# Nine portions of the attention issued beside the second query slab, and weights of feature-major slabs ordered seven pieces ahead

## The chip, the core and the metric

The kernel runs on one core of one Trainium2 chip. The metric is the device time of one execution in microseconds. A core has five engines with queues of their own: TensorE (PE in the profile; its weight loads are PEld), VectorE (DVE), ScalarE (ACT), GpSimd (POOL) and SyncE (SP), which here issues all transfers. They synchronise through semaphores, and each works through its own instructions in the order in which the program put them.

## The reference, cut to what matters

Two layers of a decoder trunk over 512 tokens of width 1024. Each layer normalises its input, multiplies it by one wide matrix, feeds two groups of heads from the columns of the product, and projects their joined outputs back:

```python
h = rms_norm(x, g_pre)
proj = jnp.einsum('bsd,de->bse', h, w_in)
q_h, f_h, i_h, z_h, q_a, k_a, v_a, z_a = jnp.split(proj, SPLIT_POINTS, axis=-1)
o_h = hgrn2(q_h, f_h, i_h, lb)                       # gated linear recurrence, 8 heads of 128
o_h = rms_norm(o_h, g_head).reshape(B, S, HG_WIDTH) * silu(z_h)
q_a = rotary(q_a ...); k_a = rotary(k_a ...)
o_a = sliding_window_attention(q_a, k_a, v_a, sinks) * silu(z_a)
y = jnp.einsum('bse,ed->bsd', jnp.concatenate([o_h, o_a], axis=-1), w_out)
return x + rms_norm(y, g_post)
```

The attention has 16 query heads of width 64, in groups of eight that share one of two key and value heads. A query sees the last 128 keys, itself included, and a learned sink per head joins the softmax. It is computed in blocks of 128 queries against the 256 keys of their own block and the one before.

## The kernel before, in words

**Arithmetic.** All is float32. A weight or activation that enters a projection is split into a rounded high part and the rest, `hi` and `lo`, and `mm3` (lines 174 to 177) multiplies three combinations, so that one step of a projection is three matmuls of 128x128 by 128x512.

**Weights.** They come in pieces of 128x512 (256 KB). `w_load` (147) issues a piece's transfer on SP into one of three `raw` buffers; `w_conv` (156) casts it on ScalarE into `whi` (169) and subtracts on VectorE into `wlo` (170; for the first query slab and the keys and values every second subtraction is on GpSimd). There are nine buffers of each. A slab is eight pieces.

**Slabs and their order.** `ORDER` lists them: keys and values (`kv`), two query slabs (QA, QA+1), two slabs of inputs (IV, IV+1), then FQ slabs (forget gates and queries of two HGRN2 heads each) between gates (ZA, ZH) and pieces of the output projection. A slab is a row of `Unit`s. In a feature-major slab (the queries, FQ and ZA) the weights are the stationary operand, and each of the four units uses two pieces for its eight steps, so that buffers come free one after the other. In a token-major slab (IV, ZH, kv) all pieces serve each of the four units, and they come free only in the last one.

**Steps.** `step` (211) issues one `mm3` of the unit whose turn it is. When the one active unit is half done, a second one is started beside it and they take turns; three PSUM buffers (`pj`) hold their results. After each step `w_conv` is told how far to have ordered casts: to the beginning of the next slab, plus one piece per four steps done (in slabs of 32 steps), plus `LEAD`, 4. A unit's end calls its evacuation.

**Attention.** The evacuation of a query slab (`qa_stream`, 371) multiplies by cosines and sines on VectorE (378 to 385), combines on GpSimd (388, 389), splits into high and low (391, 392), stores both to a `stack` in DRAM and loads them back restacked into `qs[g]` (394, 397), for one of four groups `g` of four heads per two units. The tiles of `qs` have two buffers. `att_stream` (489) runs over 16 pairs of group and block of queries, and issues, with a `yield` after each portion: the scores of block i (`att_scores`: eight matmuls, masking and maxima on VectorE, exponentials on ScalarE, the product with the reciprocal sums on GpSimd), the transposes of block i−2 (`att_transpose`, with a selection by mask on GpSimd), and the values of block i−4 (`att_value`). That makes 48 portions.

**Interleaving.** `merge` (45) takes streams with a total each and always goes on with the one that has the smallest share of its total behind it. In `run` (769) steps are issued until all four groups of queries exist, two more steps follow, and then the attention, with a total of 50, is merged with the steps that remain through the first FQ slab. The HGRN2 heads follow in the same way, two by two.

**Who sets the order.** The order in which the Python code issues instructions is a priority. A scheduler at compile time gives each engine its sequence by simulating the engines, so that an instruction whose operands or buffers are not ready there can be overtaken by a later one. Matmuls that are wrapped in `pin` (all of the attention and of HGRN2) keep their issued order among one another on TensorE; those of `mm3` are not pinned.

Of the kernel before, what the change touches and what calls it, by code (L numbers as in the profile page):

```python
# [20 lines left out]
NT = SEQ // 128  # L21
KT = D_MODEL // 128
# [5 lines left out]
FLOOR = 1e-20  # L28
NSLAB = 12
QA, IV, FQ, ZA, ZH = 0, 2, 4, 8, 10  # L30

W_BUFS = 9
RAW_BUFS = 3
# [2 lines left out]
DEFER = 18  # L36
PJ, SC = 3, 3
LEAD = 4
POOL_SLABS = (QA,)
FB = 8  # L40
QB = 4
# [3 lines left out]
def merge(*streams):  # L45
    live = [[g, 0.0, float(total)] for g, total in streams]
    while live:
        s = min(live, key=lambda e: e[1] / e[2])
        try:
            s[1] += next(s[0]) or 1.0  # L50
        except StopIteration:
            live.remove(s)


def chain(*gens):
    for g in gens:
        yield from g


def drain(g):  # L60
    for _ in g:
        pass
# [3 lines left out]
def hybrid_kernel(ctx: ExitStack, tc: tile.TileContext, x, wkv, win, wout, g_pre, g_post, lbp, ghead, sinks,  # L66
# [15 lines left out]
    def pj():  # L82
        return ps.tile([P, 512], F32, tag="pj", name="pj", bufs=PJ)
# [51 lines left out]
    for key, (first, n) in slab_first.items():  # L135
        if key[0] == "kv" or key[2] in POOL_SLABS:
            on_pool.update(range(first, first + n))
    kv_pieces = {slab_first["kv", l][0] + j: l for l in range(DEPTH) for j in range(KT // 2)}
    kv_room = {0}
    ahead = {("kv", l): sum(slab_first["out", l - 1, "h1"]) for l in range(1, DEPTH)}  # L140
    for l in range(DEPTH - 1):
        ahead["out", l, "h1"] = sum(slab_first["out", l, "h1"]) - KT - LEAD
    raws = {}
# [3 lines left out]
    def w_load(n):  # L147
        while state["raw"] < min(n, len(pieces)):
            i = state["raw"]
            src = pieces[i]  # L150
            t = wp.tile([P, 512], F32, tag="raw", name="raw", bufs=RAW_BUFS)
            nc.sync.dma_start(t.rearrange("p (a c) -> p a c", a=2) if len(src.shape) == 3 else t, src)
            raws[i] = t
            state["raw"] += 1

    def w_conv(n):
        w_load(n)
        while state["conv"] < min(n, len(pieces)):
            i = state["conv"]
            if i in kv_pieces and kv_pieces[i] not in kv_room:  # L160
                return
            w_load(i + RAW_BUFS)
            v = raws.pop(i)
            if i in kv_pieces:
                hi, lo = (big.tile([P, 512], F32R, tag="v", name="wkv", bufs=8) for _ in range(2))
            else:
                hi = wp.tile([P, 512], F32R, tag="whi", name="whi")
                lo = wp.tile([P, 512], F32R, tag="wlo", name="wlo")
            nc.scalar.copy(hi, v)  # L169
            (nc.gpsimd if i in on_pool and i % 2 else nc.vector).tensor_tensor(lo, v, hi.bitcast(F32), op=ALU.subtract)  # L170
            conv[i] = (hi, lo)
            state["conv"] += 1

    def mm3(o, sta, mov, start, stop):
        nc.tensor.matmul(o, lhsT=sta[1], rhs=mov[0], start=start, stop=False)  # L175
        nc.tensor.matmul(o, lhsT=sta[0], rhs=mov[1], start=False, stop=False)  # L176
        nc.tensor.matmul(o, lhsT=sta[0], rhs=mov[0], start=False, stop=stop)  # L177
# [8 lines left out]
    def run_first():  # L186
        _, key, fn = waiting.pop(0)
        fn()
        emitted.add(key)

    def ensure(key):
        while key not in emitted:
            run_first()
# [8 lines left out]
    units, active, turn, slab_steps, slab_done = deque(), [], [0], {}, {}  # L202
# [8 lines left out]
    def step():  # L211
        if not active or (len(active) == 1 and units and 2 * (len(active[0].ks) - active[0].i) <= len(active[0].ks)):
            u = units.popleft()
            first, n = slab_first[u.key]
            w_conv(first + n)
            u.w = [conv[first + j] for j in range(n)]
            for key in u.needs:
                ensure(key)
            u.o = pj()[:, 0:u.ncol]
            active.append(u)  # L220
        u = active[turn[0] % len(active)]
        turn[0] += 1
        k = u.ks[u.i]
        mm3(u.o, u.sta(k, u.w), u.mov(k, u.w), u.i == 0, u.i == len(u.ks) - 1)
        u.i += 1
        for e in waiting:
            e[0] -= 1
        while waiting and waiting[0][0] <= 0:
            run_first()
        slab_done[u.key] += 1  # L230
        first, n = slab_first[u.key]
        w_conv(ahead.get(u.key, first + n) + slab_done[u.key] * KT // slab_steps[u.key] + LEAD)
        if u.i == len(u.ks):
            active.remove(u)
            u.evac(u.o)

    def remaining(key):
        return sum(len(u.ks) - u.i for u in list(active) + list(units) if slab_first[u.key][0] <= slab_first[key][0])

    def through(key):  # L240
        while slab_done[key] < slab_steps[key]:
            step()
            yield 1.0

    def until(cond):
        while not cond():
            step()
# [76 lines left out]
    def layer(l, last):  # L324
# [44 lines left out]
        qs = {}  # L369
# [82 lines left out]
        def att_transpose(g, n, pt, odd):  # L452
            T = sc()
            for h in range(4):
                pin(nc.tensor.transpose(T[:, h * P:(h + 1) * P], pt[:, h * P:(h + 1) * P], ident))  # L455
            tt_ = tmp("a", F32R, 2)
            split_psum(tt_[:, 0], tt_[:, 1], T)
            if n == 0:
                return [(n, tt_[:, 0]), (n, tt_[:, 1])]
            terms = []  # L460
            for which in range(2):
                if which == 0:
                    d = big.tile([P, 2, 512], F32R, tag="oy", name="pcur", bufs=6) if odd else tmp("b", F32R, 2)
                else:
                    d = big.tile([P, 2, 512], F32R, tag="q", name="pprev", bufs=QB)
                sg = -1 if which == 0 else 1
                nc.gpsimd.affine_select(out=d.rearrange("p a (h t) -> p (a h) t", h=4),
                                        in_=tt_.bitcast(F32).rearrange("p a (h t) -> p (a h) t", h=4),
                                        pattern=[[0, 8], [-sg, P]], compare_op=ALU.is_ge, fill=0.0,
                                        base=-which, channel_multiplier=sg)  # L470
                terms += [(n - which, d[:, 0]), (n - which, d[:, 1])]
            return terms
# [16 lines left out]
        def att_stream(steps):  # L489
            pts, terms = {}, {}  # L490
            n = len(steps)
            for tt in range(NT):
                ensure(("k", l, tt))
            for i in range(n + VLAG):
                if i < n:
                    until(lambda: steps[i][0] in qs)
                    pts[i] = att_scores(*steps[i])
                    yield 1.0
                if 2 <= i <= n + 1:
                    terms[i - 2] = att_transpose(*steps[i - 2], pts.pop(i - 2), i % 2)  # L500
                    yield 1.0
                if i >= VLAG:
                    att_value(*steps[i - VLAG], terms.pop(i - VLAG))
                    yield 1.0
# [264 lines left out]
        def run():  # L769
            hg = lambda a: (hgrn(a), HG_N)  # L770
            rest = lambda key: (through(key), remaining(key))
            until(lambda: 3 in qs)
            for _ in range(2):
                step()
            merge((att_stream([(g, n) for g in range(4) for n in range(NT)]), 50), rest(("in", l, FQ)))
            merge(hg(0), rest(("in", l, FQ + 1)))
            merge(hg(2), rest(("in", l, FQ + 2)))
            merge(hg(4), rest(("out", l, "a1")))
            merge(hg(6), rest(("out", l, "h0")))
            kv_room.add(l + 1)  # L780
            drain(through(("out", l, "h1")))
# [129 lines left out]
```

## Time and profile before

| | |
|---|---|
| median of three runs | 956.77 us (952.09 to 960.68) |
| the profiled execution | 954.91 us, its span 953.2 us |
| TensorE busy | 918.9 us, 96% |
| VectorE busy | 681.9 us, 72% |
| ScalarE busy | 475.2 us, 50% |
| GpSimd busy | 267.3 us, 28% |
| mean granted TensorE clock | 0.989 |
| HBM read, written | 87.52 MB, 12.58 MB |

The span is the stretch from the first to the last instruction of the program in one profiled execution. Busy times are unions of instructions' durations. In the rows of the profile, L169 is line 169 of the kernel; a group's row ends with the idle time of its engine just before its instructions and with what ended it; in a row of the order of time the same stands in brackets. A row of the windows gives, for a stretch of the span, the busy time and the number of instructions of each engine, then the granted clock of TensorE as a share of full speed, the share of the DMA engines and GB/s. SPq is the queue of transfers on SyncE.

### The profile page before, as it was taken

The page shows a single profiled execution, that of the slowest core. Times are in us where ns is not written, and L with a number is a line of the kernel's source. Part 1 is how long each engine was busy: PE and PEld are TensorE (multiplying, and loading weights), DVE is VectorE, ACT ScalarE, POOL GpSimd, SP SyncE. Part 2 cuts the span into 40 slices and gives each one's busy share as a digit, 9 for nine tenths or more (in the row PEclk, how much of TensorE's full clock was granted, in tenths as well). Part 3 has the DMA queues.
Part 4 walks back from the last instruction along what each step waited for, and adds up shares of the span by engine and source line. Part 5 has one row for each costly group of instructions (what it writes and reads, how often), then busy time and mean ns, then how long its engine had stood idle before and what let it go on. Part 6 is the DMA issues. An engine that isn't in the chain of part 4 may idle for free.

```text
span 953.2 us, 19110 instructions
## 1 busy us (share of the span) xinstructions
PE 918.9 (96%) x7228; PEld 754.8 (79%) x7228; DVE 681.9 (72%) x1382; ACT 475.2 (50%) x1135; POOL 267.3 (28%) x282
## 2 busy tenths in 40 slices
PE   7999998999999999999969989989999999999996
PEld 5887887778878788788868878877788887887885
DVE  5866878796766685865795678778867578749546
ACT  5524766836464462434553257677363645414242
POOL 2232454422231221311331235434322213113102
PEclk8999999999999999999999999999999999999999
DMA  6456622232222332323443665122222233413313
GB/s 219 145 177 175 186 72 79 66 90 68 78 79 81 87 112 89 112 69 118 132 158 123 178 180 150 54 70 67 90 67 69 88 89 84 129 55 103 89 46 132
DMA packets 56716, 101.34 MB, mean 106 GB/s; under 512 B 6448, under 2 KB 8880, under 8 KB 56624
## 3 DMA queue, kind: packets, MB, share of 16 engines
q1 hardware_dynamic: 56624, 100.12, 35.5%
q8 instruction: 57, 0.93, 0.4%
q14 instruction: 35, 0.29, 0.1%
HBM read 87.52 MB, written 12.58 MB: 105 GB/s over the span
## 4 chain that ended last, share of the span: by engine, by line
PE 77%; DVE 9%; ACT 6%; issue 4%; POOL 2%; DMA 1%; SPq 0%; DVEq 0%; POOLq 0%; ACTq 0%
PE pj L175 22%; PE pj L177 21%; PE pj L176 21%; DVE wlo L170 3%; ACT s L442 2%; PE sc L583 2%; PE sc L428 2%; PE ac L652 1%; PE ac L481 1%; PE ac L640 1%; ACT whi L169 1%; PE ac L655 1%; DVE xn L306 1%; PE sc L455 1%; PE sc L700 1%
## 5 line engine op out<-in xcount | busy, mean ns | idle before, releaser
L169 ACT CAST whi<-raw 128x512 fp32r<-128x512 f32 x256 | 158.2, 620 | 193.5 <-PE pj L177 154.3
L170 DVE TENSOR_TENSOR wlo<-raw,whi 128x512 fp32r<-128x512 f32 x248 | 185.4, 753 | 63.0 <-ACT whi L169 61.0
L175 PE MATMUL pj<-hhi,wlo 128*128 128x512 f32 x512 | 206.4, 403 | 0.0
L177 PE MATMUL pj<-hhi,whi 128*128 128x512 f32 x512 | 200.8, 392 | 0.0
L176 PE MATMUL pj<-hlo,whi 128*128 128x512 f32 x512 | 200.2, 391 | 0.0
L177 PEld LDWEIGHTS pj<-hhi,whi 128*128 128x128 f32 x512 | 96.6, 189 | 21.0
L175 PEld LDWEIGHTS pj<-hhi,wlo 128*128 128x128 f32 x512 | 96.6, 189 | 18.7
L176 PEld LDWEIGHTS pj<-hlo,whi 128*128 128x128 f32 x512 | 96.8, 189 | 18.2
L175 PE MATMUL pj<-whi,hlo 128*128 128x512 f32 x256 | 103.2, 405 | 3.6 <-ACT whi L169 3.6
L175 PE MATMUL pj<-whi,ops 128*128 128x512 f32 x256 | 103.8, 406 | 0.0
L176 PE MATMUL pj<-wlo,hhi 128*128 128x512 f32 x256 | 100.4, 392 | 0.0
L177 PE MATMUL pj<-whi,ops 128*128 128x512 f32 x256 | 100.1, 391 | 0.0
L177 PE MATMUL pj<-whi,hhi 128*128 128x512 f32 x256 | 100.1, 391 | 0.0
L176 PE MATMUL pj<-wlo,ops 128*128 128x512 f32 x256 | 99.7, 390 | 0.0
L601 POOL TENSOR_TENSOR k<-k,tot 128x256 f32<-128x256 f32 x80 | 65.0, 832 | 109.9 <-PE sc L583 64.0
L175 PEld LDWEIGHTS pj<-whi,hlo 128*128 128x128 f32 x256 | 48.2, 188 | 12.6 <-ACT whi L169 4.5
L449 POOL TENSOR_TENSOR s<-s,sums 128x512 f32<-128x512 f32 x32 | 34.9, 1091 | 81.9 <-DVE sums L447 34.3
L177 PEld LDWEIGHTS pj<-whi,ops 128*128 128x128 f32 x256 | 48.0, 188 | 10.7
L600 DVE TENSOR_TENSOR q<-q,tot 128x256 f32<-128x256 f32 x80 | 46.9, 614 | 13.1 <-PE sc L583 8.6
L177 PEld LDWEIGHTS pj<-whi,hhi 128*128 128x128 f32 x256 | 48.1, 188 | 10.1
L175 PEld LDWEIGHTS pj<-whi,ops 128*128 128x128 f32 x256 | 48.1, 188 | 9.3
L176 PEld LDWEIGHTS pj<-wlo,ops 128*128 128x128 f32 x256 | 48.2, 188 | 9.0
(172 smaller groups left out, 1587.0 us busy)
## 6 DMA issues: line engine op xcount, KB each, us to landing
raw<-in_win_dram SPq DMA_DIRECT2D x192, 256.0 KB, 2.7
raw<-in_wout_dram SPq DMA_DIRECT2D x64, 256.0 KB, 2.7
stack<-rot SPq DMA_DIRECT2D x16, 512.0 KB, 3.9
qs<-stack SPq DMA_DIRECT2D x32, 256.0 KB, 4.4
a<-in_x_dram SPq DMA_DIRECT2D x12, 256.0 KB, 3.1
raw<-in_wkv_dram SPq DMA_DIRECT2D x8, 256.0 KB, 4.0
x_mid<-a SPq DMA_DIRECT2D x8, 256.0 KB, 2.1
a<-x_mid SPq DMA_DIRECT2D x8, 256.0 KB, 3.2
```

The source lines that it names most:

```text
L169: nc.scalar.copy(hi, v)
L170: (nc.gpsimd if i in on_pool and i % 2 else nc.vector).tensor_tensor(lo, v, hi.bitcast(F32), op=ALU.subtract)
L175: nc.tensor.matmul(o, lhsT=sta[1], rhs=mov[0], start=start, stop=False)
L176: nc.tensor.matmul(o, lhsT=sta[0], rhs=mov[1], start=False, stop=False)
L177: nc.tensor.matmul(o, lhsT=sta[0], rhs=mov[0], start=False, stop=stop)
L306: nc.vector.scalar_tensor_tensor(xn, xt[c], r, g[c], op0=ALU.mult, op1=ALU.mult)
L428: pin(nc.tensor.matmul(S[:, h * 256:(h + 1) * 256], lhsT=q[:, 2 * hp_ + h, t_], rhs=kst[v][p][:, (n - 1) * P:(n + 1) * P], start=(h == 0 a ...
L442: nc.scalar.activation(pt[:, h * P:(h + 1) * P], cur[h], AF.Exp, bias=negm[:, h:h + 1], scale=SCALE, accum_out=sums[:, h:h + 1])
L449: nc.gpsimd.tensor_tensor(pv, pv, sums.unsqueeze(2).broadcast_to([P, 4, P]), op=ALU.mult)
L583: pin(nc.tensor.matmul(L[32 * b:32 * b + 32, c:c + 16], lhsT=k[:, o_:o_ + 32], rhs=qv[:, blk:blk + qu, 1, :], start=True, stop=True, tile_ ...
L600: nc.vector.tensor_tensor(qv[:, :, 1, :], qv[:, :, 1, :], tv[:, :, 0].unsqueeze(2).broadcast_to([P, nb, hh]), op=ALU.mult)
L601: nc.gpsimd.tensor_tensor(kv_[:, :, 0, :], kv_[:, :, 0, :], tv[:, :, 1].unsqueeze(2).broadcast_to([P, nb, hh]), op=ALU.mult)
```

## The change

Attention starts when the first query slab has delivered its two groups (`1 in qs`): its first nine portions are merged with the remaining steps of the second query slab. The rest, with a total of 41, is merged as before with the steps through the first FQ slab, after the fourth group exists and two more steps. Independently, while a feature-major input slab is being computed, `w_conv` is told to order casts seven pieces ahead instead of four. Slabs of the output projection and token-major slabs keep four.

```diff
+FEATURE = (0, 1, 4, 5, 6, 7, 8, 9)
...
 LEAD = 4
+FEAT_LEAD = 7
+ATT_FIRST = 9
...
+def part(gen, n):
+    for _ in range(n):
+        yield next(gen)
...
-        w_conv(ahead.get(u.key, first + n) + slab_done[u.key] * KT // slab_steps[u.key] + LEAD)
+        w_conv(ahead.get(u.key, first + n) + slab_done[u.key] * KT // slab_steps[u.key]
+               + (FEAT_LEAD if u.key[0] == "in" and u.key[2] in FEATURE else LEAD))
...
             rest = lambda key: (through(key), remaining(key))
+            until(lambda: 1 in qs)
+            att = att_stream([(g, n) for g in range(4) for n in range(NT)])
+            merge((part(att, ATT_FIRST), ATT_FIRST), rest(("in", l, QA + 1)))
             until(lambda: 3 in qs)
             for _ in range(2):
                 step()
-            merge((att_stream([(g, n) for g in range(4) for n in range(NT)]), 50), rest(("in", l, FQ)))
+            merge((att, 50 - ATT_FIRST), rest(("in", l, FQ)))
```

## The prediction, made before the changed kernel was run

> **What bounds the kernel now.** I read the page first, for the busy shares and their course.
>
> ```profile
> span 953.2 us, 19110 instructions
> ## 1 busy us (share of the span) xinstructions
> PE 918.9 (96%) x7228; PEld 754.8 (79%) x7228; DVE 681.9 (72%) x1382; ACT 475.2 (50%) x1135; POOL 267.3 (28%) x282
> ```
>
> TensorE is busy 96% of the span and VectorE 72%. So only TensorE's idle time, or time in which it runs slower, can be won: 953.2 − 918.9 = 34 us of idle time at the most. To see where it lies I went to windows. They put the attention of the first layer beside its neighbours; I cut them at the ends of slabs (57 to 79 is the second query slab, 79 to 188 the attention beside IV, IV+1 and FQ, then HGRN2).
>
> ```profile
> core 0: us, PE busy (x) PEld busy (x) DVE busy (x) ACT busy (x) POOL busy (x), PEclk, DMA share, GB/s
> 57.00:79.00 22.00, 22.00 (x98) 18.22 (x98) 14.52 (x19) 6.01 (x10) 6.46 (x4) 1.00 0.61 171
> 79.00:90.00 11.00, 9.59 (x50) 7.88 (x50) 7.35 (x20) 5.67 (x23) 4.22 (x4) 1.00 0.41 129
> 90.00:137.00 47.00, 46.42 (x253) 38.60 (x252) 38.09 (x100) 31.04 (x112) 22.84 (x22) 1.00 0.52 141
> 137.00:160.00 23.00, 20.08 (x104) 16.79 (x103) 21.10 (x42) 14.68 (x45) 10.21 (x9) 0.96 0.37 104
> 160.00:188.00 28.00, 27.47 (x128) 21.61 (x127) 19.21 (x40) 23.23 (x49) 11.29 (x10) 0.97 0.18 57
> 188.00:474.00 286.00, 285.60 (x2737) 234.02 (x2736) 199.68 (x382) 131.52 (x267) 64.82 (x79) 1.00 0.31 92
> ```
>
> Beside the second query slab TensorE is full and VectorE two thirds busy (14.52 of 22 us). From 137 to 160 it is the other way round: VectorE 21.10 of 23 us, and TensorE has lost 2.9 us. After 188 almost nothing is lost. The order of time, TensorE alone, shows the large gaps, two in each layer and in both at the same place:
>
> ```profile
> 89.34 0.50 PE L175 MATMUL pj<-whi,hlo 128*128 128x512 f32 x1 [1.41 <-ACT whi L169]
> ...
> 158.63 0.58 PE L428 MATMUL sc<-kst,qs 128*128 128x256 f32 x1 [2.55 <-ACT s L442]
> ...
> 558.77 0.50 PE L175 MATMUL pj<-whi,hlo 128*128 128x512 f32 x1 [2.22 <-ACT whi L169]
> ...
> 628.07 0.38 PE L428 MATMUL sc<-kst,qs 128*128 128x256 f32 x1 [2.57 <-ACT s L442]
> ```
>
> The first of each pair waits for a weight cast right after IV has begun (1.41 and 2.22 us), the second has scores waiting for the exponentials of earlier scores, whose PSUM they need (2.55 and 2.57 us). Around the second kind the clock column drops too:
>
> ```profile
> 158.10:161.50 3.40, 2.87 (x11) 2.67 (x12) 2.77 (x8) 1.27 (x9) 0.99 (x2) 0.50 0.18 63
> 629.20:632.50 3.30, 3.30 (x12) 2.71 (x11) 2.05 (x8) 0.13 (x1) 1.04 (x1) 0.50 0.03 7
> ```
>
> In these two stretches TensorE was granted half its clock. 2.87 and 3.30 us of work at half speed would have taken half of that, so 1.44 and 1.65 us went. All that this change can win in these places: 1.41 + 2.22 + 2.55 + 2.57 + 1.44 + 1.65 = 11.8 us. The gaps at the start, between the layers and at the end are not touched by it.
>
> **The change, part by part.** No instruction's work is added or removed: the same 16 blocks of scores, transposes and values per layer are issued, nine portions of them earlier, and the casts, subtractions and loads of weights earlier in the program. The price is where they stand in each engine's order.
>
> First, what moves. A portion is a `yield` of `att_stream`. The first nine are scores 0, scores 1, scores 2, transpose 0, scores 3, transpose 1, scores 4, transpose 2, value 0. When `qs[1]` exists some 28 of the second slab's 32 steps are left (the pairing of units has begun its first unit), so a portion comes every 28/9 = 3.1 steps. The other 41 share the steps that 50 had: one block of the attention per 6.7 steps instead of 5.5, 0.82 of the density. VectorE's part of a block comes from its groups from 79 to 188 us:
>
> ```profile
> L170 DVE TENSOR_TENSOR wlo<-raw,whi 128x512 fp32r<-128x512 f32 x26 | 22.1, 863 | 2.8 <-ACT whi L169 2.3
> L487 DVE TENSOR_TENSOR oa<-ac,u 64x256 f32<-64x256 f32 x28 | 11.6, 413 | 2.5 <-ACT u L483 2.1
> L268 DVE TENSOR_TENSOR a<-sc,a 128x512 fp32r<-128x512 f32 x16 | 10.9, 683 | 1.4 <-ACT a L267 1.0
> L432 DVE COPY_PREDICATED sc<-masks,sc 128x256 f32<-128x256 uint8 x24 | 9.7, 421 | 3.1 <-PE sc L428 3.0
> L433 DVE TENSOR_REDUCE mx<-sc 128x2 f32<-128x256 f32 x24 | 9.5, 415 | 0.1
> ```
>
> The small operations of a block of scores (there are four) are read from one of them, with its least, median and longest duration in ns:
>
> ```profile
> L436 DVE SCALAR_TENSOR_TENSOR negm<-mx,nsnk x16: 142/156/1042, 85.0 to 168.5; 128x4 f32<-128x4 f32 x16
> ```
>
> A block of scores costs two predicated copies (0.42 each), two maxima (0.415), and four small operations at 0.16: 2.3 us. A transpose costs 0.68, a value 2 × 0.41 = 0.83. Moved: 5 × 2.3 + 3 × 0.68 + 0.83 = 14.4 us of VectorE per layer.
>
> **The stall in the scores.** From 137 to 160 stand some four blocks of scores, transposes and values, 4 × (2.3 + 0.68 + 0.83) = 15.2 us, and the subtractions of the slab that follows IV+1, ten at 0.86 us. At 0.82 of the density the blocks take 12.5: VectorE gets 2.7 us back in this stretch, against a stall of 2.55. I take both stalls as gone (5.1 us), and the halved clock with them (3.1). The wider lead helps here too: FQ is feature-major, so the next slab's subtractions are ordered ahead of more of the attention.
>
> **A rule that speaks on this.** The trace has the halved clock start at 158.1, with a gap of 2.55 us; a gap of 2.22 us in the other layer left the clock alone. The Trainium skill, "TensorE: Matmul & The Clock Gate", under "Why this matters for your kernels", asks for idle gaps above about 3 us before the clock falls. By that rule a 2.55 us gap would not be the cause, the 3.1 us would stay, and the sum would end at 952; the trace does not agree with it, and the row decides.
>
> **The stall at the start of IV.** ScalarE is busy with the first two blocks of exponentials when IV's last two pieces should be cast:
>
> ```profile
> 88.57 0.21 ACT L445 ACTIVATE es<-ds 128x4 f32<-128x4 f32 x1
> 88.66 1.66 ACT L169 CAST whi<-raw 128x512 fp32r<-128x512 f32 x3
> ```
>
> The casts at 88.66 follow directly on the exponentials, and TensorE goes on at 89.34. With the change these two blocks' exponentials stand some 20 us earlier, where ScalarE has 6.01 of 22 us busy, and with the lead of seven these two pieces (6 and 7 of IV) are ordered at the slab's steps 0 and 4, by the formula in `step`, instead of 12 and 16. I take both gaps as gone, 3.6 us. If another block of scores stands there instead, they stay.
>
> **What it costs.** The cover for the moved work is the idle VectorE beside the second slab:
>
> ```profile
> L384 DVE TENSOR_TENSOR rot<-pj,cs 128x512 f32<-128x512 f32 x3 | 2.1, 692 | 9.9 <-PE pj L177 9.9
> ```
>
> 9.9 us of it is idle time before the rotary multiplications, which wait for TensorE. The demand becomes 14.52 + 14.4 = 28.9 us. The time to do it in grows by TensorE's own moved work:
>
> ```profile
> 125.43 1.11 PE L428 MATMUL sc<-kst,qs 128*128 128x256 f32 x8
> 126.38 0.40 PE L175 MATMUL pj<-whi,hlo 128*128 128x512 f32 x1
> ...
> 127.77 0.60 PE L455 MATMUL sc<-ident,s 128*128 128x128 f32 x4
> 128.13 0.47 PE L175 MATMUL pj<-whi,hlo 128*128 128x512 f32 x1
> ```
>
> The next matmul starts 0.95 us after a block of scores and 0.36 us after a block of transposes; a step of the slab takes 22.00 × 3/98 = 0.67 us, and the first value, two matmuls wide as a slab's, two thirds of that. 5 × 0.95 + 3 × 0.36 + 0.45 = 6.3 us, so 28.3 us. VectorE would be full, somewhat worse than its 0.92 from 137 to 160, where 2.55 us and 1.44 of clock were lost. Bounds of a new stall: nothing, if the excess slides into IV, where the load has just fallen; or one stall like that, 4.0 us per layer, 8.0 in all. I take the middle, 4.0, because the second slab's units hold three PSUM buffers with two in use, so an evacuation may be late by most of a unit before TensorE notices.
>
> GpSimd's part comes along: five multiplications and four selections beside the rotary work. In the trace such an operation costs VectorE time:
>
> ```profile
> 156.70 1.04 DVE L436 SCALAR_TENSOR_TENSOR negm<-mx,nsnk 128x4 f32<-128x4 f32 x1
> ...
> 156.25 1.48 POOL L467 TENSOR_SCALAR_AFFINE_SELECT pcur<-a 128x1024 fp32r<-128x1024 f32 x1 [3.15 <-DVE a L268]
> ```
>
> A 128x4 operation took 1.04 us beside the selection, against its median of 0.16. The Trainium skill, "SBUF — State Buffer", under "Who interferes with whom", says that a VectorE instruction with two SBUF inputs and a GpSimd instruction that reads SBUF exclude each other for a whole instruction. The trace agrees here. It speaks against the change, since the second slab's subtractions and rotary splits have two SBUF inputs and beside them stood only four GpSimd operations until now: if every one of nine moved operations blocked 0.9 us, 8 us of VectorE would be added per layer, the stall would be the upper bound, 8.0 instead of 4.0, and the sum 951 as profiled.
>
> On SP's queue the loads are ordered earlier as well. Here they can't start earlier, since each waits for a raw buffer that a subtraction frees, so I cost that at nothing; what it does to the queries stands in the first rival.
>
> **The sum.** −3.6 − 5.1 − 3.1 + 4.0 = −7.8 us against the profiled execution's 954.91: 947.1. That execution lies 1.9 us under the median of the runs (956.77), so the forecast is 949, 0.8% faster.
>
> **Rivals.**
>
> *The second group's queries come too late (slower).* Scores 4 is the seventh portion and the first to read `qs[1]`. It is issued after 6 × 3.1 = 18.7 steps of 0.67 us and 4 × 0.95 + 2 × 0.36 us of attention: 57 + 12.5 + 4.5 = 74. The SP queue of before:
>
> ```profile
> 70.55 0.33 SPq L152 DMA_DIRECT2D raw<-in_win_dram  x1
> 70.93 0.43 SPq L394 DMA_DIRECT2D stack<-rot  x1
> 71.46 5.61 SPq L397 DMA_DIRECT2D qs<-stack  x4
> ```
>
> The second store of this group's queries stands behind a weight load that waited for its buffer until 70.55, the four loads of `qs` are issued from 71.46 on over 5.61 us, and landing takes
>
> ```profile
> DMA to landing us min/median/max: 3.1/4.3/6.1
> ```
>
> so the last lands near 80.5. If TensorE's order has scores 4 at 74, all slab matmuls behind it wait 6.5 us, and longer loads in front of the store make it worse. With the clock (1.6 us) that is 8.1 us per layer, 16.2; the gap in front of IV goes (3.6), the later one stays: 954.9 + 12.6 + 1.9 = 969. Against it: matmuls of slabs aren't pinned, so the program's order may have put them ahead of scores 4 if the queries were expected late. From a wait of 5 us per layer on it decides: 2 × (5 + 1.6) − 3.6 = 9.6 us, 1% of the time. Chance 0.13.
>
> *VectorE is the bound of the second slab.* The upper end, 8.0, and the gap at the start of IV stays because IV's subtractions are late in the full queue: −5.1 − 3.1 + 8.0 = −0.2, so 956 to 957. For it the 28.9 us in 28.3; against it the slack of PSUM. Chance 0.25.
>
> *Nothing new stalls.* −11.8: 943 as profiled, 945 as a median. For it the 2.7 us that VectorE wins where it is scarce; against it the full second slab. Chance 0.17.
>
> *The change does not do what it says:* the portions and casts are issued earlier but each engine's order comes out nearly as before, as the casts wait for whi buffers anyway. 955 to 957. Chance 0.08.
>
> **How the numbers follow.** The forecast's own chance is 0.37, with 945 to 953 as its range. A measurement of this kernel can tell about 1% from no change (the three runs lie from 952.09 to 960.68). Faster by over 1% is below 947.2: most of the third rival and under half of the forecast, 0.32. Slower by over 1% is above 966.3: the first rival, 0.12. Within 1%: 0.56. The range goes from 941 (nothing new stalls, and some smaller gaps go too) to 964, which leaves out most of the first rival.
>
> **What would show it.** Right: no gap over 1 us on TensorE in front of a weight cast near the start of IV; none before scores near the end of IV+1, and no half clock there; VectorE over 0.9 busy beside the second slab and under 0.85 from 137 to 160, counted from the same place in the slabs. Wrong: a gap in front of the fifth block of scores with the queries' loads landing just before it; a halved clock inside the second slab; rotary multiplications of the second slab that start late with TensorE waiting for a projection's PSUM; or the same two gaps as before, moved by the few microseconds that TensorE's moved work takes.

## The result and the profile after

The changed kernel takes 962.65 us (median of 19 runs, 960.71 to 966.31), the kernel before 957.96 in the same series (19 runs, 952.09 to 960.68). The ratio is 1.0058 with an interval of 1.0043 to 1.0073: 0.6% slower. That lies within 1% and inside the range, but the forecast of 949 had the wrong sign.

The page of the changed kernel, its first lines:

```profile
span 963.6 us, 19111 instructions
## 1 busy us (share of the span) xinstructions
PE 922.3 (96%) x7228; PEld 756.9 (79%) x7228; DVE 687.5 (71%) x1382; ACT 469.0 (49%) x1131; POOL 267.9 (28%) x282
```

The span grew by 10.4 us against the profile of before. Of that 922.3 − 918.9 = 3.4 us is longer busy time of TensorE with the same 7228 matmuls, most of it a lower clock, and 7.0 us is idle time (41.3 against 34.3). Part of the difference is spread between runs: the profiled execution of before took 954.91 us, below its median, and that of the changed kernel 965.34, above its own. The medians are 4.7 us apart.

The same windows as before, cut at the same places of the program; the moved blocks make the second query slab last from 59 to 90 (31 us instead of 22):

```profile
core 0: us, PE busy (x) PEld busy (x) DVE busy (x) ACT busy (x) POOL busy (x), PEclk, DMA share, GB/s
59.00:90.00 31.00, 28.40 (x143) 23.23 (x142) 23.98 (x50) 14.57 (x47) 10.66 (x8) 1.00 0.62 167
90.00:99.00 9.00, 8.66 (x48) 6.95 (x47) 5.92 (x12) 2.86 (x10) 7.22 (x8) 1.00 0.44 147
99.00:146.00 47.00, 41.92 (x198) 34.33 (x197) 34.01 (x81) 24.92 (x88) 17.46 (x15) 0.89 0.43 113
146.00:170.00 24.00, 24.00 (x126) 20.27 (x125) 18.31 (x44) 14.97 (x46) 10.35 (x9) 1.00 0.30 78
```

VectorE did not fill up: 23.98 of 31 us is 0.77. TensorE lost 2.60 us there, and 5.1 us in the 47 us after 99, where before it lost 0.6 in a window of the same length, and there the clock column reads 0.89. From 146 to 170, the place of the late stall of before, TensorE is full and VectorE at 18.31 of 24, 0.76. So the late stall went from there, and something else came. The order of time on TensorE gives the gaps by name, in brackets the idle time and what ended it; of the ten beside the attention that last 0.8 us or more, six are shown:

```profile
79.64 0.39 PE L437 MATMUL sc<-kst,qs 128*128 128x256 f32 x1 [1.69 <-ACT s L451]
...
104.13 0.58 PE L437 MATMUL sc<-kst,qs 128*128 128x256 f32 x1 [3.54 <-ACT s L451]
...
135.71 0.38 PE L437 MATMUL sc<-kst,qs 128*128 128x256 f32 x1 [1.54 <-ACT s L451]
...
568.74 0.50 PE L183 MATMUL pj<-whi,hlo 128*128 128x512 f32 x1 [1.48 <-DVE rot L388]
...
578.48 0.38 PE L437 MATMUL sc<-kst,qs 128*128 128x256 f32 x1 [2.10 <-ACT s L451]
...
662.21 0.50 PE L490 MATMUL ac<-pcur,vst 128*128 128x512 f32 x1 [1.37 <-POOL pcur L476]
```

And the two stretches at half clock, by windows:

```profile
103.00:109.80 6.80, 5.67 (x17) 4.70 (x18) 2.85 (x10) 3.74 (x19) 1.04 (x1) 0.50 0.59 126
137.20:140.60 3.40, 3.40 (x11) 2.72 (x10) 2.47 (x8) 0.90 (x5) 0.88 (x1) 0.50 0.00 0
```

9.07 us of work at half speed cost 4.5 us, all in the first layer; before it was 1.44 + 1.65 = 3.1 in both.

Neither layer waits for a weight cast any more. Instead the first burst of scores waits for its own exponentials, 1.69 us at 79.64, 0.80 at 85.68 and, in the second layer, 1.44 at 556.81. The late gap before scores has shrunk to 1.54 us (135.71; 1.55 at 608.30) and stands earlier. New are 3.54 and 2.10 us before scores in the middle, 1.48 us before a projection whose PSUM a rotary multiplication had not yet emptied, and 1.37 us (662.21; 1.34 at 191.22) before values near the end, behind a selection of GpSimd.

Where do the 3.54 us come from? The order of time around it, on four engines:

```profile
95.18 1.01 PE L426 MATMUL sc<-kst,qs 128*128 128x128 f32 x8
...
95.11 1.09 POOL L476 TENSOR_SCALAR_AFFINE_SELECT b<-a 128x1024 fp32r<-128x1024 f32 x1
96.16 1.54 POOL L476 TENSOR_SCALAR_AFFINE_SELECT pprev<-a 128x1024 fp32r<-128x1024 f32 x1
97.68 1.29 POOL L398 TENSOR_TENSOR rot<-rot 128x512 f32<-128x512 f32 x1
...
98.99 0.62 ACT L400 CAST rot<-rot 128x512 fp32r<-128x512 f32 x1 [2.69 <-POOL rot L398]
...
99.65 0.91 DVE L401 TENSOR_TENSOR rot<-rot 128x512 fp32r<-128x512 f32 x1 [2.29 <-ACT rot L400]
100.47 0.74 DVE L429 COPY_PREDICATED_SCALAR sc<-masks,neg 128x512 f32 x1
```

Read it from the bottom. The scores at 104.13 wait for exponentials, these for the maxima, and these for the mask, L429, at 100.47, although the scores that it masks were started at 95.18. VectorE works through its queue in order, and ahead of the mask stands the second rotary split, L401, for which VectorE had sat idle for 2.29 us; it waits for ScalarE's cast L400, which sat idle for 2.69 us until GpSimd's combination L398. GpSimd had ended the first combination at 95.1, and the last multiplication that the second needs began at 93.79 and took 0.68 us; but two selections of the moved attention were queued ahead, from 95.11 to 97.68. They hold the combination up by 2.6 us, and VectorE, idle for 2.29 us ahead of the split, could have had the mask that much earlier. So by this reading up to 2.3 of the 3.54 us are two selections on an engine that is busy 28% of the time, passed on by engines that each work in their own order. In the second layer the maximum behind the mask stands behind such a split in the same way (2.10 us). I call this the queue order (C in the later expectations). Its rivals: that VectorE or GpSimd simply have too much work there (plain load), that scores lack PSUM buffers (D in the expectations), and that the wider lead of the weights is to blame alone.

### The profile page after: what moved, and what is told of

The parts are those of the page before. It is cut to its first block, busy times and chain, and to the rows that moved or that the text cites. A ratio compares the mean times of both kernels' runs of the same rounds, so it can differ in the third digit from the quotient of the medians.

```text
span 963.6 us, 19111 instructions
## 1 busy us (share of the span) xinstructions
PE 922.3 (96%) x7228; PEld 756.9 (79%) x7228; DVE 687.5 (71%) x1382; ACT 469.0 (49%) x1131; POOL 267.9 (28%) x282
## 3 DMA queue, kind: packets, MB, share of 16 engines
q1 hardware_dynamic: 56624, 100.12, 35.7%
## 4 chain that ended last, share of the span: by engine, by line
PE 70%; DVE 10%; ACT 5%; issue 3%; POOL 3%; DMA 0%; DVEq 0%; POOLq 0%; ACTq 0%
PE pj L183 20%; PE pj L185 19%; PE pj L184 19%; DVE wlo L178 3%; PE sc L592 2%; ACT s L451 2%; PE sc L437 2%; PE ac L661 1%; PE ac L649 1%; ACT whi L177 1%; PE ac L490 1%; PE ac L664 1%; PE sc L709 1%; DVE oa L496 1%; DVE sc L441 1%
## 5 line engine op out<-in xcount | busy, mean ns | idle before, releaser
L451 ACT ACTIVATE s<-sc,negm 128x128 f32<-128x128 f32 x128 | 45.6, 369 | 37.2 <-DVE negm L445 31.8
L458 POOL TENSOR_TENSOR s<-s,sums 128x512 f32<-128x512 f32 x32 | 34.7, 1086 | 88.1 <-DVE sums L456 34.9
L185 PEld LDWEIGHTS pj<-whi,hhi 128*128 128x128 f32 x256 | 48.8, 191 | 10.4
L185 PEld LDWEIGHTS pj<-whi,ops 128*128 128x128 f32 x256 | 48.0, 188 | 10.7
L184 PEld LDWEIGHTS pj<-wlo,hhi 128*128 128x128 f32 x256 | 49.0, 191 | 8.3
```

What stands on the lines that cost most here:

```text
L451: nc.scalar.activation(pt[:, h * P:(h + 1) * P], cur[h], AF.Exp, bias=negm[:, h:h + 1], scale=SCALE, accum_out=sums[:, h:h + 1])
L458: nc.gpsimd.tensor_tensor(pv, pv, sums.unsqueeze(2).broadcast_to([P, 4, P]), op=ALU.mult)
```

## The experiments

Each kernel ran beside the kernel before on the same chip. Together (median us; ratio to before with its 95% interval; TensorE's idle time, the span less its busy time on the page, in the one profiled execution of each, which scatters by some us). The experiments ran in three series, in which the kernel before had medians of 956.88, 956.35 and 957.29 us; each ratio is to the one of its own series:

| kernel | median | ratio | idle |
|---|---|---|---|
| before | 957.96 | 1 | 34.3 |
| after | 962.65 | 1.0058 (1.0043 to 1.0073) | 41.3 |
| early attention alone | 956.52 | 0.9998 (0.9981 to 1.0016) | 36.3 |
| wider lead alone | 957.58 | 0.9996 (0.9979 to 1.0014) | 34.3 |
| after, combinations on VectorE | 956.49 | 0.9991 (0.9977 to 1.0006) | 34.9 |
| after, 5 portions | 960.69 | 1.0034 (1.0020 to 1.0049) | 36.8 |
| after, rotary chain first | 959.88 | 1.0037 (1.0022 to 1.0051) | 37.9 |
| after, 4 buffers for scores | 962.59 | 1.0068 (1.0045 to 1.0091) | 41.8 |
| before, 4 buffers for scores | 973.19 | 1.0176 (1.0150 to 1.0202) | 50.4 |
| early attention, combinations on VectorE | 950.59 | 0.9943 (0.9922 to 0.9964) | 32.6 |
| before, combinations on VectorE | 959.00 | 1.0008 (0.9989 to 1.0027) | 38.1 |
| after, 6 portions and a pause | 954.38 | 0.9961 (0.9944 to 0.9977) | 34.0 |
| early attention, 6 portions, pause, combinations on VectorE | 951.73 | 0.9929 (0.9908 to 0.9951) | 32.6 |

**The two parts, each alone.** First the early attention without the lead:

```
-FEAT_LEAD = 7
+FEAT_LEAD = 4
```

> The early attention without the wider lead. Theory A (rotary chain): what costs time is that GpSimd's selections of the moved attention stand in front of the rotary combinations of the second query slab, and ScalarE and VectorE wait for these with scores queued behind them. Then this is slower than before like the changed kernel, 1.003 to 1.008, with a gap of over 2 us in front of the scores that follow scores 4. Theory B (lead): what costs time is that weight loads ordered seven ahead stand in front of the loads of the queries on SP (the first group's last load landed at 68.6 instead of 61.1), so that the first blocks of scores are bunched. Then this is at 0.990 to 1.000 of before, the first group's queries land near 61, and no gap over 1 us stands in front of scores inside the second slab.

Then the lead without the early attention (the three added lines of `run()` taken out, and the `merge` of before in its old place):

```
-            until(lambda: 1 in qs)
-            att = att_stream([(g, n) for g in range(4) for n in range(NT)])
-            merge((part(att, ATT_FIRST), ATT_FIRST), rest(("in", l, QA + 1)))
```

> The wider lead without the early attention. A: nothing of the attention stands beside the rotary work, the gap of 1.4 and 2.2 us at the start of IV shrinks, 0.994 to 1.001 of before. B: slower than before, 1.003 to 1.007, as loads of the queries come later. My prediction had taken both gaps at the start of IV as gone through this part among others.

Neither moves the time: 0.9998 and 0.9996. The 0.6% needs both, so the lead as the sole cause falls. With the lead alone the order of time shows a wait for scores where the wait for a cast had been, 1.84 us at 87.74, and the late gap untouched:

```profile
159.75 0.58 PE L437 MATMUL sc<-kst,qs 128*128 128x256 f32 x1 [2.57 <-ACT s L451]
```

With the early attention alone the order around the second rotary group is another one than after:

```profile
89.40 1.30 POOL L397 TENSOR_TENSOR rot<-rot 128x512 f32<-128x512 f32 x1 [1.58 <-DVE sums L455]
90.66 1.29 POOL L398 TENSOR_TENSOR rot<-rot 128x512 f32<-128x512 f32 x1
...
90.36 1.00 PE L426 MATMUL sc<-kst,qs 128*128 128x128 f32 x8
...
93.86 1.57 DVE L178 TENSOR_TENSOR wlo<-raw,whi 128x512 fp32r<-128x512 f32 x1
95.36 0.74 DVE L429 COPY_PREDICATED_SCALAR sc<-masks,neg 128x512 f32 x1
```

The combinations follow each other directly, ahead of the selections (93.35). The mask comes at 95.36, still 5.0 us after its scores (90.36), but now VectorE is busy until then, with the splits and, from 93.86 on, 1.57 us of a weight subtraction. That subtraction stands beside the selection of 93.35, and the two behind it take 0.92 and 0.68 us. So here it is VectorE's own work, and it is cheaper: the waits of TensorE before the scores that follow are 2.08 us (100.12) and 0.56 us (569.4) in the two layers, against 3.54 and 2.10. Two waits of 1.16 us for late subtractions, before projections (95.49 and 563.78), come with it.

**The combinations away from GpSimd.** In the changed kernel the two rotary combinations go to VectorE:

```
-                nc.gpsimd.tensor_tensor(a[:, 0], a[:, 0], b[:, 0], op=ALU.subtract)
-                nc.gpsimd.tensor_tensor(b[:, 1], b[:, 1], a[:, 1], op=ALU.add)
+                nc.vector.tensor_tensor(a[:, 0], a[:, 0], b[:, 0], op=ALU.subtract)
+                nc.vector.tensor_tensor(b[:, 1], b[:, 1], a[:, 1], op=ALU.add)
```

> The changed kernel with the two rotary combinations per group on VectorE instead of GpSimd (some 4 x 2 x 0.7 us more on VectorE per layer). A: the rotary chain no longer waits for selections, the gaps of 3.5 and 2.1 us and the halved clock behind them go: 5 to 8 us faster than the changed kernel, 0.997 to 1.001 of before. B: the queries' loads are as late as before, VectorE has more to do: 1.004 to 1.009.

0.9991: the whole loss is gone although VectorE was given more work. A VectorE that is short of time, my price for the change, would have become worse; as far as VectorE is meant, plain load falls as the cause of the loss. The wait in the middle is 2.13 us instead of 3.54, and 1.76 instead of 2.10. More than that went at the start of the attention, where 1.69, 0.80 and 1.44 us had been lost and now no wait of over 0.5 us is left. The mask of the first block stands behind the rotary chain of another group there. First the changed kernel, then this version:

```profile
72.72 1.29 POOL L398 TENSOR_TENSOR rot<-rot 128x512 f32<-128x512 f32 x1
...
75.91 0.75 DVE L429 COPY_PREDICATED_SCALAR sc<-masks,neg 128x512 f32 x1
```

```profile
70.64 0.68 DVE L398 TENSOR_TENSOR rot<-rot 128x512 f32<-128x512 f32 x1
...
73.22 0.75 DVE L429 COPY_PREDICATED_SCALAR sc<-masks,neg 128x512 f32 x1
```

The mask follows its scores after 2.9 us in the changed kernel (72.97) and 1.2 us here (72.01). No selection is queued there; the two combinations took 1.77 and 1.29 us on GpSimd and 0.68 us each on VectorE. So this run speaks against GpSimd in the rotary chain, but it does not part the selections ahead of it from its longer operations.

**Fewer portions.**

```
-ATT_FIRST = 9
+ATT_FIRST = 5
```

> The changed kernel with five portions beside the second slab instead of nine: scores 0 to 3 and one transpose, none of which has a selection on GpSimd. A: no selection stands in front of the rotary combinations, so the gaps near scores 4 and 5 go: 0.996 to 1.001 of before. B: the lead is the same, 1.004 to 1.008.

1.0034, and the wait in the middle is still there, 3.24 and 3.25 us. The fifth block of scores stood at almost the same place, at 91.94, and its mask stood behind a different instruction that waited for GpSimd through ScalarE:

```profile
95.03 0.59 ACT L276 CAST a<-sc 128x512 fp32r<-128x512 f32 x1 [3.28 <-POOL pprev L476]
...
95.65 0.69 DVE L277 TENSOR_TENSOR a<-sc,a 128x512 fp32r<-128x512 f32 x1 [2.60 <-ACT a L276]
96.26 0.74 DVE L429 COPY_PREDICATED_SCALAR sc<-masks,neg 128x512 f32 x1
```

So five portions don't take the attention out of the way; the combination is not the only thing that can be caught, the kind of chain is the same.

**The rotary chain issued first.** The five lines from the combinations to the splits are put ahead in each engine's order:

```
+                with tc.high_priority(200):
                     nc.gpsimd.tensor_tensor(a[:, 0], ...)
                     ...
                         nc.vector.tensor_tensor(r.bitcast(F32R), r, h, op=ALU.subtract)
```

> The changed kernel with the rotary combinations and splits at a higher priority, so that the last group's two combinations on GpSimd stand in front of the selections and one behind the other. Theory C (queues): the gaps of 3.5 and 2.1 us come from scores 4's mask, which stands in VectorE's order behind the last rotary split, and the split waits for GpSimd behind selections. Then these gaps shrink to under 1.5 us and the kernel is 2 to 4 us faster than the changed one, 1.001 to 1.004 of before. Theory D (PSUM): three buffers for scores are too few for any delay of some us, whatever causes it; then the gaps stay over 2 us, and 1.004 to 1.007.

Half an answer, 1.0037. In the first layer the combinations now precede the selections and the wait fell from 3.54 to 1.37 us. In the second a selection at 564.53 still stood between the two (563.30 and 565.59), and the wait there was 2.57 us, against 2.10. The hand on the order reached one layer only, so the time can't speak for or against the queue order.

**PSUM for scores.** A fourth buffer for scores, paid for with one accumulator less, in the changed kernel and in the kernel before:

```
-PJ, SC = 3, 3
+PJ, SC = 3, 4
```

> The changed kernel with four PSUM buffers for scores and transposes instead of three, taken from the values (one accumulator instead of two). D: scores no longer wait for the exponentials of the block before, the gaps of 1.7, 3.5 and 1.5 us in front of scores go, and the kernel is 5 to 10 us faster than the changed one, 0.995 to 1.001 of before, less what the single accumulator costs. C: the mask is as late as before, scores 5 wait less by one half block of scores, about 1 us per gap: 1.002 to 1.005.

> The kernel before with four PSUM buffers for scores instead of three, one accumulator for values. D: its gaps of 2.55 and 2.57 us in front of scores and the halved clock behind them go too, 4 to 8 us: 0.992 to 0.997. C: these gaps have another cause than the rotary split (VectorE is full there), so up to half of them goes, 0.997 to 1.002; the single accumulator may cost as much.

1.0068 and 1.0176. The late gap before scores in the kernel before, which by D had to shrink, did not (2.55 before):

```profile
162.85 0.74 PE L428 MATMUL sc<-kst,qs 128*128 128x256 f32 x4 [2.89 <-ACT s L442]
```

D falls for that gap. For the changed kernel the run is not conclusive: in the middle scores no longer wait, as D said, but transposes do, 1.86 us in one layer (100.06, ended by the addition of values on VectorE) and 3.48 in the other (571.80), and the missing accumulator may add waits of its own.

**Early attention without both suspects.** The lead back at four and the combinations on VectorE (the two edits shown above):

> The early attention without the wider lead (no difference from before when alone) and the rotary combinations on VectorE (which took the changed kernel back to before). C: both remove waits of scores behind the rotary work, in part the same ones, so 0.994 to 1.000. D: neither adds a buffer, 0.998 to 1.002.

0.9943, the first version that beats the kernel before: 950.59 us. The page's first lines:

```profile
span 951.0 us, 19092 instructions
## 1 busy us (share of the span) xinstructions
PE 918.4 (97%) x7228; PEld 754.9 (79%) x7228; DVE 682.2 (72%) x1398; ACT 468.2 (49%) x1131; POOL 241.8 (25%) x266
```

1.7 us less idle time than before, and no half clock inside either attention. One row of this trace limits the reading by queue order: the mask of the fifth block comes late here as well, at 97.29, 5.1 us after its scores (92.21). But TensorE sat idle only 0.15 us in front of the scores that follow at 100.95: its order had other matmuls there for nearly all of the time. (A wait of 1.24 us stands a little earlier, at 95.42, before a projection whose weights were cast late.) A late mask costs only what TensorE's order did not fill. That the combinations on VectorE are not a gain by themselves had to be shown:

> The kernel before with the rotary combinations on VectorE instead of GpSimd, and nothing else. The early attention with these combinations and without the wider lead was at 0.9943 of before. If the gain is the combinations' own (a shorter chain, whatever stands beside it), this is at 0.993 to 0.997. Theory C has it come from both together: before, no scores stand behind the first three groups' rotary work, so moving it is worth little alone, 0.997 to 1.001.

1.0008: in the kernel before they are worth nothing. This gain needs the early attention, a GpSimd that doesn't stand between it and the rotary chain, and the lead at four.

The four versions with nine portions ahead make a square, and it prices both suspects. The lead of seven costs 1.0058 − 0.9998 = 0.60% with the combinations on GpSimd and 0.9991 − 0.9943 = 0.48% with them on VectorE. The combinations on GpSimd cost 0.67% with the lead of seven and 0.55% with four. In each of these pairs the intervals lie apart, and neither price depends visibly on the other suspect. So the lead's harm does not go through the combinations on GpSimd. The waits of TensorE above 0.5 us beside the attention, in the one profile of each and both layers together, show the places (in us; start is up to 15 us behind the first scores, middle up to 50, late up to 100):

| kernel | start | middle | late | last values |
|---|---|---|---|---|
| before | 3.6 (weight casts) | 0 | 5.1 | 0 |
| after | 3.9 | 7.8 | 3.1 | 2.7 |
| early attention alone | 3.4 | 5.8 | 0.7 | 2.8 |
| after, combinations on VectorE | 0 | 6.6 | 2.5 | 2.7 |
| early attention, combinations on VectorE | 1.5 | 3.7 | 0 | 2.7 |
| after, 6 portions and a pause (below) | 3.1 | 0 | 6.6 | 0 |

The lead's price stands in the middle (2.0 and 2.9 us) and late (2.4 and 2.5 us), that of the combinations on GpSimd at the start (3.9 and 1.9 us) and in the middle (1.2 and 2.1 us).

**A pause around the chain, with GpSimd and the lead kept.** If the queue order is right, nothing has to be moved to another engine: it is enough that no selection is issued while the second rotary group is in flight. Six portions go ahead, and twelve steps of the slabs without attention follow:

```
-ATT_FIRST = 9
+ATT_FIRST = 6
...
-            for _ in range(2):
+            for _ in range(12):
                 step()
```

> The changed kernel with six portions beside the second slab and twelve steps instead of two before the rest, so that scores 4 come when the last group's rotary work is done; GpSimd and the lead as changed. Theory C (scores 4's mask stands behind the last rotary split, which waits for GpSimd): the gaps of 3.5 and 2.1 us go to under 1 us, 0.999 to 1.004 of before, as the rest of the attention is denser. A theory of plain load (VectorE and ScalarE have too much to do near there) says that a gap over 2 us stays, only later: 1.004 to 1.008.

0.9961, better than I had expected. The order of time at the place of the 3.54 us:

```profile
90.89 1.29 POOL L397 TENSOR_TENSOR rot<-rot 128x512 f32<-128x512 f32 x1
92.14 1.28 POOL L398 TENSOR_TENSOR rot<-rot 128x512 f32<-128x512 f32 x1
...
92.87 2.56 DVE L401 TENSOR_TENSOR rot<-rot 128x512 fp32r<-128x512 f32 x2 [0.46 <-ACT rot L400]
...
96.55 0.75 DVE L429 COPY_PREDICATED_SCALAR sc<-masks,neg 128x512 f32 x1 [1.12 <-PE sc L426]
```

Combination follows combination, the two splits come together, and now VectorE waits for the scores (1.12 us, ended by TensorE), the mask following its scores (95.51) after 1.0 us. No gap above 0.5 us is left on TensorE between 79 and 150. GpSimd and VectorE have the same instructions to do as in the changed kernel, at another time, and are busy about as long (269.2 and 686.9 us, against 267.9 and 687.5). So neither the amount of work nor operations that slow each other down explain the loss, and the order of issue is shown as its cause: 8.3 us between the medians come from it alone. Which part of the order is not parted. The pause lets the combination go first, but it also spreads the scores that follow over more time, and a wait of some 2 us was left in the middle in the two versions in which only the second combination was no longer held up (2.08 with the lead at four, 2.13 with the combinations on VectorE). That two selections in particular are up to 2.3 us is read from the trace of the changed kernel, not measured apart. Against the kernel before only part of this is explained: its idle time on the page is about the same (34.0 and 34.3) and both late gaps with their half clock are there, so the 0.4% that it gains I can't assign to places.

**Both.** Pause of eight steps, six portions, lead four, combinations on VectorE:

> Early attention without the wider lead, rotary combinations on VectorE, six portions beside the second slab and eight steps before the rest. C: beside e8_att_only_rot_dve (0.9943) the remaining gaps of 1.2 and 0.75 us near scores 4 shrink: 0.991 to 0.995. Plain load: the rest of the attention is denser, 0.995 to 1.000.

0.9929 (0.9908 to 0.9951), 951.73 us. Its interval overlaps that of the version without the pause, 0.9922 to 0.9964: once the combinations no longer queue on GpSimd, the pause adds nothing that can be told. These two are the best versions.

## Why the prediction was wrong

*The stall at the start of IV, 3.6 us to be won.* Half right. No cast is waited for. But I wrote that if another block of scores stands there, the gaps stay, and one does: 1.69 + 0.80 + 1.44 = 3.9 us in place of 3.6, and the start of the attention costs such a gap in the lead-alone version too (1.84 us). It need not: with the combinations on VectorE, and with them the first mask 1.2 us behind its scores, none of over 0.5 us is left.

*The stall in the scores, 5.1 us to be won, and 3.1 of clock.* The mechanism was right, VectorE is relieved late (0.76 instead of 0.92), but two gaps of 1.5 us remain, so 2.0 us were won. With the lead at four one of 0.74 us remains, and none with the combinations on VectorE besides. So the wider lead, which I had counted as a help in this place, works against it. The clock was lost at other places, 4.5 us instead of 3.1.

*What it costs, 4.0 us, bounds 0 and 8, and nothing for the lead.* This is the step that failed. It looked for the price in VectorE's load, and the square has it elsewhere: the combinations on GpSimd cost 0.55 to 0.67% (5.3 to 6.4 us of 957) and the lead 0.48 to 0.60% (4.6 to 5.7 us), beside the moved attention only. Without both, the early attention is 0.57% faster, not far from the 0.8% of the forecast. I compared 28.9 us of VectorE's work with 28.3 us of time and took VectorE as full. It was busy 0.77 of the slab's 31 us, and just behind them (90 to 99) 5.92 of 9, idle in front of instructions that waited for GpSimd by way of ScalarE. The new gaps that the order of time names come to 3.54 + 2.10 + 1.48 + 1.34 + 1.37 = 9.8 us. I had moved GpSimd's five multiplications and four selections along and priced them only by what they take from VectorE beside them; I had not asked what stands behind them in GpSimd's own queue, the rotary combinations of the very slab that the attention was moved into. That an operation of VectorE gets longer beside a selection was seen again, at the remaining late gap and before the gap of 1.48 us at 568.74:

```profile
133.77 1.04 DVE L445 SCALAR_TENSOR_TENSOR negm<-mx,nsnk 128x4 f32<-128x4 f32 x1
...
565.03 1.48 DVE L178 TENSOR_TENSOR wlo<-raw,whi 128x512 fp32r<-128x512 f32 x1 [0.16 <-ACT whi L177]
566.44 1.04 DVE L447 TENSOR_TENSOR ds<-snk,negm 128x4 f32<-128x4 f32 x1
```

Beside the first stands a selection (133.32, 1.48 us). The 0.9 us more than the usual 0.15 lie in front of exponentials for which TensorE waited 1.54 us. Beside the other two stand selections from 564.88 to 567.47; against 0.68 and 0.15 us elsewhere they are 1.7 us longer, just ahead of the multiplication for which TensorE waited. So that gap is of the kind that I had priced; it is what such collisions cost, and not what decided.

*SP's queue, at nothing.* The order of the loads did change. The loads of the first group's queries went out in one stretch before, from 53.68 to 56.57; with the wider lead weight loads, each waiting for its buffer, are queued between them:

```profile
55.99 0.33 SPq L406 DMA_DIRECT2D qs<-stack  x1
56.47 0.38 SPq L160 DMA_DIRECT2D raw<-in_win_dram  x1
57.61 0.32 SPq L406 DMA_DIRECT2D qs<-stack  x1
60.76 2.04 SPq L160 DMA_DIRECT2D raw<-in_win_dram  x2
62.84 0.91 SPq L406 DMA_DIRECT2D qs<-stack  x2
```

The last two of the four were issued at 62.84 to 63.75, 7.2 us later. The scores of the first block began at 72.97, with the early attention alone at 69.6. But with the lead at four and the combinations on VectorE they began at 72.62, although the last of these loads was issued at 59.41. So it isn't shown that the late loads set this start, or that they are the lead's price. With the lead alone they cost nothing (0.9996): nobody wants the queries yet.

*The rivals.* The second group's queries were not waited for: their last load landed at 85.96, and scores 4 stood at 95.18. VectorE as the bound came nearest to the time (956 to 957) with the wrong mechanism. The gap at 568.74, TensorE before a projection whose PSUM waits for a late rotary multiplication, is of the kind that I listed as a sign of error; it was a smaller part.

*The sum again, from the trace.* Idle time 41.3 − 34.3 = +7.0, and longer busy time +3.4: +10.4 in place of −7.8 for one pair of profiles, and +4.7 between medians. Of the 3.4 only 4.5 − 3.1 = 1.4 us lie in the attention. Half clock at the start and between the layers makes up some 0.8 more; the rest of TensorE's longer busy time is not accounted for.

What stays open: the gaps of 1.34 and 1.37 us before the last values were not tried by themselves. How the lead does its harm is open too. It is not through the combinations on GpSimd, since it costs as much without them there, and it needs the early attention (0.9996 without). The pause leaves the lead in and is fast, but it moves the attention as well.

## What to carry to other kernels

Before one stream of work is moved beside another, list for each engine what of the new stream will stand ahead of the old one's chain, the hardly used engines first: an engine at 28% can hold up one at 96% when two others wait for it in order. A sum of busy times against a window can't see this; the rows to read are an idle time "ended by" a different engine, followed upstream until an engine is found that was busy with something else. Where such a chain is found, an empty stretch in the moved stream costs nothing to try and may be worth as much as moving work to another engine. And two parts of a change are to be run in a square, each with and without the other: the lead was harmless alone and cost half a percent beside the moved attention.

## What the runs showed of the hardware

The half clock did not follow the length of the gap alone. In the changed kernel the gap of 3.54 us that ended at 104.13 began at 100.6, and the granted clock was already half from 103.0, 2.4 us into it, and for 6.8 us; a gap of 1.54 us (135.71) was followed by half clock from 137.2 on for 3.4 us, and one of 2.10 us (578.48) by none. So a gap of 2 us may cost nothing or, by 3.40 us at half speed, 1.7 us more. The Trainium skill, "TensorE: Matmul & The Clock Gate", under "Why this matters for your kernels", sets the danger at idle gaps above about 3 us; the traces here differ for 1.54 and, in the kernel before, 2.55, and in the gap of 3.54 us the clock was half before 3 us had passed.
